# Nine norms' sums in four column groups of the array, and two stretches of vector work held in program order

## The chip, the cores and the metric

The kernel runs on one core of a Trainium2 chip. The metric is the device time of one execution in microseconds (us); less is better. Engines are called PE (matrix multiplications), DVE (vector), ACT (scalar functions and copies), POOL (a second, slower vector engine) and SP (which issues most DMA transfers). Each runs its own instructions in its own order and waits for the others through semaphores. SBUF is the on-chip memory, PSUM holds matmul results in eight banks of 128 partitions by 512 floats.

## The reference

One step of a decoder layer, in float32, over 1024 prompt tokens and 8 x 4 sample tokens, 1024 channels. Cut to what matters:

```python
def _rms(x, g):
    return x * lax.rsqrt(jnp.mean(x * x, axis=-1, keepdims=True) + EPS) * g

def _layer(x, p, attn_fn, ...):
    h = _rms(x, n_mix_pre)
    z = h @ w_in                                   # q | k | v | u
    a, k_state, v_state = attn_fn(q, k, v)         # window 128, a learned sink per head
    m, pool_state = _pool_mixer(u, ...)
    mix = jnp.concatenate([a, m], axis=-1) @ w_out
    x = x + _rms(mix, n_mix_post)
    f = _rms(x, n_ffn_pre)
    f = (jax.nn.silu(f @ w_gate) * (f @ w_up)) @ w_down
    x = x + _rms(f, n_ffn_post)
    return x + jax.nn.sigmoid(x @ w_ple_gate) * (p @ w_ple), ...

def _sink_attention(q, k, v, mask, sinks):
    s = jnp.where(mask, q @ k.T * 64 ** -0.5, -jnp.inf)
    m = jnp.maximum(s.max(-1), sink)
    e = jnp.exp(s - m)
    return (e / (e.sum(-1) + jnp.exp(sink - m))) @ v
```

There are four norms for each token. In the sample's attention ("decode") the scores of one kv head are 128 rows by 1056 keys: 8 caches of 128 and 32 new ones.

## The kernel before

**Layout.** Activations lie with channels in partitions and tokens in columns. The 1056 tokens are three groups of 352 columns; group 2 holds the decode tokens at its end. Each large GEMM is done as three products of values split in a high and a low half (`split`: ACT casts the high part, DVE subtracts it, L173 and L174): high x high, low x high, high x low, each with 128x128 weights and 352 columns on PE (L128). Names end in h and l for the halves: `fh`, `fl` are the FFN's input, `wh`, `wl` weights, `hid` and `hp` the hidden activations, `sh`, `sl` sums of weights. For groups 0 and 1 the FFN uses a scheme of seven products of sums (`seven`, `do_dn_pair`), whose sums of weights are made by POOL (L1058), and whose results DVE adds up from PSUM (L1085, L1228: `p`, `u`, `c`, `ap`).

**What sets the order.** PE's order is the order in which the program is written. Transfers by SP and PSUM banks follow it: a bank is given out in turn, and a matmul that gets one waits until the result eight banks ago has been read. DVE, ACT and POOL instructions are ordered by a scheduler at build time, except where `fix` is called while `fixed[0]` is true: then the instruction keeps its place in the program. Work that accompanies the GEMMs (norms, splits, reloads) is written as generators, called chains. After each product `turn(n)` advances a clock by n matmuls, and resumes each chain that is due; a chain says with `yield load, wait` how much DVE work it has just issued and how long it then waits, both in matmuls (0.16 us in the profile).

**Norms.** `rstd_steps(acc)` gets the squares summed down to one 128 x 352 tile. Three matmuls with `acc`'s columns as weights and one column of ones as moving data give sums in token order, 128 x 3 (the last piece overlaps). ACT takes the root, DVE the reciprocal, and splits it in halves (`hl`); two multiplies with shifted identities (`diag`) make a 128 x 384 matrix `dg` of each half, and after `yield 6, 14` two matmuls with ones as weights spread the result over all partitions. It is used twelve times: three times at the start, six in `ffn_steps`, three in `x2_steps` after the FFN.

**Decode softmax.** `dscores` makes the scores of two kv heads (`a_1322`, `a_1323`) and calls `softmax` for each: maximum, its negative `nmx`, the sink's part `es`, the exponent with its sum on ACT, sum and reciprocal on DVE, the multiply on POOL (L707). `scores` then does the same for a prompt block, of two times four heads (`a_1366`); its masked copies are an ACT copy and a DVE copy by predicate (L741, L742). `dturned` transposes the weights on PE (L122), and between these stand filler products: `out_pool`, whose result ACT copies to `y` (L844). Later come `dvalues`, in column groups of 64.

**Reload.** Group 2's FFN input was stored in DRAM. `do_reload` issues two loads of it (`fr`, 128 x 1408 each) and starts a chain which splits each into `fh` and `fl` while the last down projections of the seven products run; `do_combine` ends that stretch by finishing all chains.

Of the kernel before, what the change touches and what calls it, by code (L numbers as in the profile page):

```python
# [16 lines left out]
P = 128  # L17
# [45 lines left out]
def trunk_kernel(  # L63
# [68 lines left out]
    def bank():  # L132
        return psum.tile([P, 512], F32, tag="b", name=nm("b"))
# [218 lines left out]
            for k in range(KC)  # L352
        ]

    def rstd_steps(acc):

        n = acc.shape[1]
        sm = bank()  # L360
        for i in range(TB):
            at = min(i * P, n - P)
            mm(sm[:, i : i + 1], acc[:, at : at + P], ones[:, 0:1], start=True, stop=True)
        sd = spool.tile([P, TB], F32, tag="sd", name=nm("sd"))
        fix(se.activation(sd, sm[:, :TB], AF.Sqrt, bias=epst, scale=1.0 / D))
        fix(ve.reciprocal(sd, sd))
        hl = spool.tile([P, 2, TB], F32R, tag="hl", name=nm("hl"))
        fix(ve.tensor_copy(hl[:, 0], sd))
        fix(ve.tensor_tensor(hl[:, 1], sd, hl[:, 0].bitcast(F32), op=ALU.subtract))
        dgs = []  # L370
        dg2 = act_tile([P, 2, TB, P], F32R, "dg")
        for h in range(2):
            dg = dg2[:, h]
            fix(
                ve.tensor_tensor(
                    dg, diag, hl[:, h].bitcast(F32).unsqueeze(2).to_broadcast([P, TB, P]), op=ALU.mult
                )
            )
# [169 lines left out]

    pinned[0] = True
    norms = [None] * G  # L550
    norms[0] = rstd_steps(acc1[0])
    for h in range(2):
        for c in range(4):
            u_prod(c, 0, h)
# [11 lines left out]
    x_operand(2, 1)  # L566
    for c in range(4):
        u_prod(c, 1, 1)
    norms[1] = rstd_steps(acc1[1])
    u_norm(norms[1], 1)  # L570
    for h in range(2):
        u_prod(0, 2, h)
# [4 lines left out]
        u_evict(c, 1)  # L577
        se.copy(u_decode(c)[:, :, 0:PST], stt[:, c])
    split(wplh, wpll, wpl)
    norms[2] = rstd_steps(acc1[2])  # L580
    u_norm(norms[2], 2)
    for h in range(2):
        u_prod(1, 2, h)
# [103 lines left out]
            ve.tensor_tensor(lo[:, :, dst], src, hi[:, :, dst].bitcast(F32), op=ALU.subtract)  # L687
            at += m

    def softmax(t, nh, scale, sk, nsk):  # L690

        mx = spool.tile([P, nh], F32, tag="mx", name=nm("mx"))
        ve.tensor_reduce(mx, t, axis=AX.X, op=ALU.max)
        nmx = spool.tile([P, nh], F32, tag="nmx", name=nm("nmx"))
        ve.scalar_tensor_tensor(nmx, mx, -scale, nsk, op0=ALU.mult, op1=ALU.min)
        es = spool.tile([P, nh], F32, tag="es", name=nm("es"))
        ve.tensor_tensor(es, sk, nmx, op=ALU.add)
        se.activation(es, es, AF.Exp)
        sm = spool.tile([P, nh], F32, tag="sm", name=nm("sm"))
        for c in range(nh):  # L700
            se.activation(  # L701
                t[:, c, :], t[:, c, :], AF.Exp, bias=nmx[:, c : c + 1], scale=scale, accum_out=sm[:, c : c + 1]
            )
        ve.tensor_tensor(sm, sm, es, op=ALU.add)
        ve.reciprocal(sm, sm)
        nk = t.shape[2]
        ge.tensor_tensor(t, t, sm.unsqueeze(2).to_broadcast([P, nh, nk]), op=ALU.mult)  # L707

    def m4(i):
        return am[:, i, :].unsqueeze(1).to_broadcast([P, 4, WIN])  # L710
# [4 lines left out]
    def scores(b):  # L715


        t = act_tile([P, 8, WIN])
        nk = 2 * WIN if b else WIN
        lo = b * WIN + WIN - nk  # L720
        at = WIN * 4 // nk
        both = [[bank() for _ in range(4 // at)] for _ in range(2)]
        for c in range(4):
            for kv in range(2):
                rows = slice(64 * kv, 64 * kv + 64)
                i = c % at
                mm(
                    both[kv][c // at][:, i * nk : (i + 1) * nk],
                    qT[c][rows, b * WIN : (b + 1) * WIN],
                    kT[rows, lo : lo + nk],  # L730
                    start=True,
                    stop=True,
                )
        for kv in range(2):
            tk = t[:, 4 * kv : 4 * kv + 4, :]
            for i, ps in enumerate(both[kv]):
                tc_ = tk[:, i * at : (i + 1) * at, :]
                v = ps.rearrange("p (c k) -> p c k", k=nk)
# [7 lines left out]
            softmax(tk, 4, 0.125, skp[:, hs], nskp[:, hs])  # L746
        return t

    def turned(b, t):
# [44 lines left out]
    def dscores():  # L794
        ts = [act_tile([P, 1, NK]) for _ in range(2)]
        for lo, n in ((0, 512), (512, 512), (1024, NDEC * DSEQ)):
            for kv in range(2):
                rows = slice(64 * kv, 64 * kv + 64)
                ps = bank()
                if lo < 1024:  # L800
                    k = ckt[rows].rearrange("p b w -> p (b w)")[:, lo : lo + n]
                else:
                    k = kT[rows, SEQ:]
                mm(ps[:, :n], qd[rows], k, start=True, stop=True)
                ve.tensor_tensor(ts[kv][:, 0, lo : lo + n], ps[:, :n], dmt[:, lo : lo + n], op=ALU.add)  # L805
        for kv in range(2):
            softmax(ts[kv], 1, 0.125, skd[:, kv : kv + 1], nskd[:, kv : kv + 1])
        return ts

    def dturned(t):  # L810
# [420 lines left out]

    def do_combine():
        finish(list(chains))
        for a, b in ((2, 1), (1, 6), (7, 1), (1, 5), (1, 3), (4, 7), (7, 5)):
            ve.tensor_tensor(accp[a], accp[a], accp[b], op=ALU.add)
        os_[0] = [accp[2], accp[4]]
        os_[1] = [accp[1], accp[7]]
        for g in (0, 1):
            begun.update((g, m) for m in range(KC))
# [9 lines left out]
            nc.sync.dma_start(d, t)  # L1249

    def do_reload():
        def steps():
            ts = [half(2, s="fr") for h in range(2)]
            for h in range(2):
                nc.sync.dma_start(ts[h], fsd[h])
            yield 0, 50
            for h in range(2):
                fs[2][h] = f_operand(ts[h], 2)
                yield 10, 70

        chain(steps())

# [219 lines left out]
```

## Time and profile before

| what | value |
|---|---|
| three runs | 1088.72, 1089.14, 1089.16 us, median 1089.14 |
| the profiled execution | 1088.29 us; its span 1086.5 us |
| granted PE clock | 0.999 of full speed |
| PE busy | 1076.8 us, 99% |
| DVE, ACT, POOL busy | 873.2 (80%), 512.4 (47%), 283.2 us (26%) |
| pitch of 128x352 matmuls | 0.16 us |

The span runs from the first to the last instruction; the executed time is 1.8 us more. Rows of the timeline show the start, the duration, the engine, the line in the code, the operation, output and input by name, the shape, a count, and in brackets how long the engine had been idle and what it waited for. Matmuls are pipelined: each is shown with 0.32 us but starts 0.16 us after the one before. In the waits of PE the numbers are total us, times, and the longest. DVE is over 90% busy in several stretches of the FFN, the last of them from about 794 to 845 us, and PE waits for it in few places.

### The profile page before, as it was taken

To read this page: it belongs to the slowest core of one execution; us is meant where nothing else is said; L and a number is where in the kernel's file an instruction comes from. 1 tells how busy PE (TensorE), PEld (TensorE's weight loads), DVE (VectorE), ACT (ScalarE), POOL (GpSimd) and SP (SyncE) were. 2 spreads that over 40 slices of the span, in tenths; PEclk is the share of its full clock that TensorE was granted. 3 is DMA by queue.
4 is the path that set the end of the run, shared out by engine and by line. 5 is a ranking of instruction groups with operands and counts; after the bars stand their busy time and mean duration, and the time that the engine had idled before them with its cause. 6 is when DMAs were issued, how large, how long until landed. Compare 5 with 4: busy or idle time off the path is not lost.

```text
span 1086.5 us, 17727 instructions
## 1 busy us (share of the span) xinstructions
PE 1076.8 (99%) x6867; PEld 1060.1 (98%) x6867; DVE 873.2 (80%) x1312; ACT 512.4 (47%) x877; POOL 283.2 (26%) x212
## 2 busy tenths in 40 slices
PE   9999999999999999999999999999999999999998
PEld 8999988899999999999999999999998999999998
DVE  6777478886878956796598898898899997969973
ACT  7423277774555533345543343443344365545531
POOL 0073032200000023436545445454442000022300
PEclk9999999999999999999999999999999999999999
DMA  8121311534553432322222222212234556553461
GB/s 296 59 72 39 120 50 40 188 143 141 190 184 130 136 117 78 131 78 78 78 79 78 83 74 85 91 59 97 79 112 161 170 179 224 182 210 125 135 203 60
DMA packets 43572, 131.27 MB, mean 121 GB/s; under 512 B 5060, under 2 KB 15588, under 8 KB 43488
## 3 DMA queue, kind: packets, MB, share of 16 engines
q1 hardware_dynamic: 42160, 128.38, 34.7%
q10 hardware_dynamic: 1328, 1.77, 0.5%
q8 instruction: 54, 0.88, 0.3%
q14 instruction: 30, 0.25, 0.1%
HBM read 114.25 MB, written 15.87 MB: 120 GB/s over the span
## 4 chain that ended last, share of the span: by engine, by line
PE 95%; DVE 3%; POOL 1%; ACT 1%; issue 1%; DMA 0%; SPq 0%; DVEq 0%; POOLq 0%; ACTq 0%
PE b L128 94%; PE b L122 1%; POOL wr L1058 1%; DVE sl L174 1%; DMA xr<-in_x_dram 0%; DVE hp L174 0%; DVE a L805 0%; DVE ap L1228 0%; ACT a L701 0%; DVE wl L174 0%; DVE hf L1133 0%; POOL a L707 0%; DVE w L174 0%; ACT sh L173 0%; DVE fl L174 0%
## 5 line engine op out<-in xcount | busy, mean ns | idle before, releaser
L1058 POOL TENSOR_TENSOR wr<-wr,wr 128x512 f32<-128x512 f32 x108 | 174.0, 1625 | 482.2 <-DMA wr<-in_w_gu_dram 242.3
L173 ACT CAST wh<-wr 128x1024 fp32r<-128x1024 f32 (+1 forms) x138 | 142.1, 1031 | 164.3 <-PE b L128 92.2
L174 DVE TENSOR_TENSOR wl<-wr,wh 128x1024 fp32r<-128x1024 f32 (+1 forms) x138 | 168.1, 1219 | 51.4 <-ACT wh L173 35.4
L128 PE MATMUL b<-fh,wh 128*128 128x352 f32 x624 | 201.5, 323 | 0.0
L128 PE MATMUL b<-fh,wl 128*128 128x352 f32 x624 | 200.0, 320 | 0.0
L128 PE MATMUL b<-fl,wh 128*128 128x352 f32 x624 | 199.9, 320 | 0.0
L173 ACT CAST sh<-wr 128x1024 fp32r<-128x1024 f32 x72 | 75.7, 1051 | 138.0 <-POOL wr L1058 131.9
L128 PE MATMUL b<-fh,sh 128*128 128x352 f32 x416 | 134.3, 323 | 0.0
L128 PE MATMUL b<-fl,sh 128*128 128x352 f32 x416 | 133.2, 320 | 0.0
L128 PE MATMUL b<-fh,sl 128*128 128x352 f32 x416 | 133.2, 320 | 0.0
L174 DVE TENSOR_TENSOR sl<-wr,sh 128x1024 fp32r<-128x1024 f32 x72 | 97.5, 1356 | 36.1 <-ACT sh L173 18.2
L128 PEld LDWEIGHTS b<-fl,wh 128*128 128x128 f32 x624 | 117.4, 188 | 0.0
L128 PEld LDWEIGHTS b<-fh,wh 128*128 128x128 f32 x624 | 117.0, 188 | 0.0
L128 PEld LDWEIGHTS b<-fh,wl 128*128 128x128 f32 x624 | 116.9, 187 | 0.0
L128 PE MATMUL b<-h,wh 128*128 128x352 f32 x480 | 105.6, 326 | 0.6 <-ACT h L426 0.6
L128 PE MATMUL b<-hid,wh 128*128 128x352 f32 x416 | 99.6, 322 | 0.0
L128 PEld LDWEIGHTS b<-h,wh 128*128 128x128 f32 x480 | 82.4, 190 | 1.6 <-ACT h L426 0.9
L1058 POOL TENSOR_TENSOR wr<-wr 128x512 f32<-128x512 f32 x36 | 51.0, 1416 | 105.9 <-DVE w L174 105.9
L128 PEld LDWEIGHTS b<-fl,sh 128*128 128x128 f32 x416 | 78.2, 188 | 0.0
L128 PEld LDWEIGHTS b<-fh,sh 128*128 128x128 f32 x416 | 78.0, 188 | 0.0
L128 PEld LDWEIGHTS b<-fh,sl 128*128 128x128 f32 x416 | 77.9, 187 | 0.0
L128 PE MATMUL b<-hp,sh 128*128 128x352 f32 x320 | 76.7, 322 | 0.8 <-DVE p L1085 0.6
(195 smaller groups left out, 2245.7 us busy)
## 6 DMA issues: line engine op xcount, KB each, us to landing
wr<-in_w_gu_dram SPq DMA_DIRECT2D x88, 512.0 KB, 3.3
wr<-in_w_dn_dram SPq DMA_DIRECT2D x40, 512.0 KB, 3.2
wr<-in_w_pg_dram SPq DMA_DIRECT2D x16, 512.0 KB, 3.5
x<-in_x_dram SPq DMA_DIRECT2D x6, 704.0 KB, 9.9
x1d<-x SPq DMA_DIRECT2D x6, 704.0 KB, 3.6
x<-x1d SPq DMA_DIRECT2D x6, 704.0 KB, 5.7
out_y_dram<-yo SPq DMA_DIRECT2D x24, 176.0 KB, 1.9
wr<-in_w_out_b_dram SPq DMA_DIRECT2D x8, 512.0 KB, 3.3
```

What stands on the lines that cost most here:

```text
L122: ins = te.transpose(out, src, ident)
L128: ins = te.matmul(*args, **kw)
L173: fix(se.copy(hi, src))
L174: fix(ve.tensor_tensor(lo, src, hi.bitcast(F32), op=ALU.subtract))
L1058: ge.tensor_tensor(out, a, b, op=op)
```

## The change

**Norms.** The old function is kept as `rstd_first` for the three norms at the start. The new `rstd_steps` takes `acc` as moving data: four matmuls, each with 32 columns of ones as weights and a quarter of the tokens (88) as columns, each into its own 32 partitions of one bank. So every token's sum stands in 32 partitions. Root, reciprocal and halves are 128 x 88, and four identity columns (`lead`) pick one row of each group of 32 to build the 128 x 352 matrix. The chain yields 8, 22 there, so the two spreading matmuls stand 12 to 24 products later in some places.

**Decode softmax.** One call for both heads: first maximum, `nmx` and `es` of each, then the exponents of both, then sum, reciprocal and multiply of each, with the DVE instructions held in this order.

**Reload.** `fixed[0]` is true from `do_reload` until `do_combine`, so the two splits stand where the chain issues them, and the chain waits 75 rather than 50 matmuls after the loads, and 12 rather than 70 between the splits.

Line numbers behind the norms are 24 to 36 higher after the change (L707 becomes L739, L742 L774, L844 L875, L1228 L1261).

How the order moves on DVE in the decode softmax. `mx_1342` and the next maximum are those of the two kv heads; `b_1367` to `b_1370` are the banks of the prompt block's scores. Before:

```order
L693 TENSOR_REDUCE mx_1354<-a_1323 128x1
L695 SCALAR_TENSOR_TENSOR nmx_1344<-mx_1342,c_1290 128x1
L742 COPY_PREDICATED a_1366<-a_1280,b_1367 128x256
L697 TENSOR_TENSOR es_1346<-c_76,nmx_1344 128x1
L695 SCALAR_TENSOR_TENSOR nmx_1356<-mx_1354,c_1290 128x1
L742 COPY_PREDICATED a_1366<-a_1280,b_1368 128x256
L697 TENSOR_TENSOR es_1358<-c_76,nmx_1356 128x1
L742 COPY_PREDICATED a_1366<-a_1280,b_1369 128x256
L693 TENSOR_REDUCE mx_1383<-a_1366 128x4
L695 SCALAR_TENSOR_TENSOR nmx_1385<-mx_1383,c_1289 128x4
L704 TENSOR_TENSOR sm_1349<-sm_1349,es_1346 128x1
L705 RECIPROCAL sm_1349<-sm_1349 128x1
```

The first head's sum stood behind the first prompt maximum. Now, from the same place:

```order
L722 SCALAR_TENSOR_TENSOR nmx_1344<-mx_1342,c_1290 128x1
L774 COPY_PREDICATED a_1366<-a_1280,b_1369 128x256
L724 TENSOR_TENSOR es_1346<-c_76,nmx_1344 128x1
L720 TENSOR_REDUCE mx_1348<-a_1323 128x1
L722 SCALAR_TENSOR_TENSOR nmx_1350<-mx_1348,c_1290 128x1
L724 TENSOR_TENSOR es_1352<-c_76,nmx_1350 128x1
L736 TENSOR_TENSOR sm_1355<-sm_1355,es_1346 128x1
L737 RECIPROCAL sm_1355<-sm_1355 128x1
L736 TENSOR_TENSOR sm_1358<-sm_1358,es_1352 128x1
L737 RECIPROCAL sm_1358<-sm_1358 128x1
L774 COPY_PREDICATED a_1366<-a_1280,b_1368 128x256
L774 COPY_PREDICATED a_1366<-a_1280,b_1370 128x256
```

Both sums and reciprocals stand ahead of two of the four copies; both prompt maxima follow these copies.

The same place on ACT: the exponents of the decode head (`a_1323`), those of the prompt block (`a_1366`), and the copy of `y`, which empties the bank `b_1443`. Before:

```order
L701 ACTIVATE a_1323,sm_1361<-a_1323,nmx_1356 128x1056
L698 ACTIVATE es_1387<-es_1387 128x4
L741 COPY a_1366<-b_1370 128x256
L701 ACTIVATE a_1366,sm_1390<-a_1366,nmx_1385 128x128 x4
L844 COPY y_1287<-b_1443 128x352
L698 ACTIVATE es_1406<-es_1406 128x4
L701 ACTIVATE a_1366,sm_1409<-a_1366,nmx_1404 128x128 x4
L818 COPY a_1458<-b_1459 128x512
```

The copy of `y` stood between two fours of exponents. Now:

```order
L731 ACTIVATE a_1323,sm_1358<-a_1323,nmx_1350 128x1056
L773 COPY a_1366<-b_1368 128x256
L773 COPY a_1366<-b_1370 128x256
L173 CAST wh_1918<-wr_1225 128x1024
L731 ACTIVATE a_1366,sm_1390<-a_1366,nmx_1385 128x128 x2
L728 ACTIVATE es_1387<-es_1387 128x4
L731 ACTIVATE a_1366,sm_1390<-a_1366,nmx_1385 128x128 x2
L731 ACTIVATE a_1366,sm_1409<-a_1366,nmx_1404 128x128
L728 ACTIVATE es_1406<-es_1406 128x4
L731 ACTIVATE a_1366,sm_1409<-a_1366,nmx_1404 128x128 x3
L875 COPY y_1287<-b_1443 128x352
L849 COPY a_1458<-b_1459 128x512
```

It now stands behind all eight, and a cast of weights stands ahead of them.

The reload on ACT, where `sh_8356` is a cast of summed weights and `hid_8275` the hidden activations. Before:

```order
L173 CAST sh_8356<-wr_8154 128x1024
L173 CAST fh_8554<-fr_8458 128x1408
L173 CAST hid_8275<-c_8408 128x352
L173 CAST wh_8375<-wr_8315 128x1024
L1157 ACTIVATE p_8317<-p_8317 128x352
```

And now:

```order
L173 CAST sh_8356<-wr_8154 128x1024
L173 CAST hid_8275<-c_8408 128x352
L173 CAST wh_8375<-wr_8315 128x1024
L1190 ACTIVATE p_8317<-p_8317 128x352
```

The cast of `fr` no longer stands between the weights and `hid`; it comes seven rows further on.

The reload on DVE, at the adds of down projections (`ap`). Before:

```order
L1228 TENSOR_TENSOR ap_5237<-ap_5237,b_8531 128x352
L174 TENSOR_TENSOR fl_8555<-fr_8458,fh_8554 128x1408
L174 TENSOR_TENSOR sl_8490<-wr_8360,sh_8489 128x1024
L1228 TENSOR_TENSOR ap_5254<-ap_5254,b_8539 128x352
L1228 TENSOR_TENSOR ap_5254<-ap_5254,b_8547 128x352
```

Now at this place, and ten rows further on:

```order
L1261 TENSOR_TENSOR ap_5237<-ap_5237,b_8531 128x352
L1261 TENSOR_TENSOR ap_5254<-ap_5254,b_8539 128x352
L174 TENSOR_TENSOR sl_8490<-wr_8360,sh_8489 128x1024
L1261 TENSOR_TENSOR ap_5254<-ap_5254,b_8547 128x352
```
```order
L1261 TENSOR_TENSOR ap_5168<-ap_5168,b_8605 128x352
L174 TENSOR_TENSOR fl_8587<-fr_8458,fh_8586 128x1408
L174 TENSOR_TENSOR wl_8518<-wr_8449,wh_8517 128x1024
L1261 TENSOR_TENSOR ap_5185<-ap_5185,b_8613 128x352
L1261 TENSOR_TENSOR ap_5185<-ap_5185,b_8621 128x352
L174 TENSOR_TENSOR wl_8592<-wr_8499,wh_8591 128x1024
L174 TENSOR_TENSOR fl_8629<-fr_8459,fh_8628 128x1408
L1261 TENSOR_TENSOR ap_5216<-ap_5216,b_8639 128x352
```

The first `fl` moved behind nine of these rows, the second behind `wl_8592`.

The diff, without the rows that only rename the first three calls:

```diff
-    def rstd_steps(acc):
+    def rstd_first(acc):
...
+    def rstd_steps(acc):
+        w = acc.shape[1] // 4
+        sm = bank()
+        for j in range(4):
+            mm(sm[32 * j : 32 * j + 32, :w], ones[:, :32], acc[:, j * w : (j + 1) * w], start=True, stop=True)
+        t = act_tile([P, 10, w], F32R, "dg")
+        sd, hl = spool.tile([P, w], F32, tag="sw", name=nm("sw")), t[:, 8:10]
+        se.activation(sd, sm[:, :w], AF.Sqrt, bias=epst, scale=1.0 / D)
+        ve.reciprocal(sd, sd)
+        ve.tensor_copy(hl[:, 0], sd)
+        ve.tensor_tensor(hl[:, 1], sd, hl[:, 0].bitcast(F32), op=ALU.subtract)
+        lead = ident[:, ::32].unsqueeze(2).to_broadcast([P, 4, w])
+        for h in range(2):
+            part = hl[:, h].bitcast(F32).unsqueeze(1).to_broadcast([P, 4, w])
+            ve.tensor_tensor(t[:, 4 * h : 4 * h + 4], lead, part, op=ALU.mult)
+        yield 8, 22
+        ps = bank()
+        for h in range(2):
+            mm(ps[:, : 4 * w], ones_r, t[:, 4 * h : 4 * h + 4].rearrange("p i k -> p (i k)"), start=h == 0, stop=h == 1)
+        return ps[:, : 4 * w]
...
-    def softmax(t, nh, scale, sk, nsk):
...
+    def softmax(*parts):
+        scale = 0.125
+        held = []
+        for t, nh, sk, nsk in parts:
+            mx = spool.tile([P, nh], F32, tag="mx", name=nm("mx"))
+            fix(ve.tensor_reduce(mx, t, axis=AX.X, op=ALU.max))
+            nmx = spool.tile([P, nh], F32, tag="nmx", name=nm("nmx"))
+            fix(ve.scalar_tensor_tensor(nmx, mx, -scale, nsk, op0=ALU.mult, op1=ALU.min))
+            es = spool.tile([P, nh], F32, tag="es", name=nm("es"))
+            fix(ve.tensor_tensor(es, sk, nmx, op=ALU.add))
+            held.append((nmx, es))
+        sums = []
+        for (t, nh, _, _), (nmx, es) in zip(parts, held):
+            se.activation(es, es, AF.Exp)
+            sm = spool.tile([P, nh], F32, tag="sm", name=nm("sm"))
+            for c in range(nh):
+                se.activation(
+                    t[:, c, :], t[:, c, :], AF.Exp, bias=nmx[:, c : c + 1], scale=scale, accum_out=sm[:, c : c + 1]
+                )
+            sums.append(sm)
+        for (t, nh, _, _), (_, es), sm in zip(parts, held, sums):
+            fix(ve.tensor_tensor(sm, sm, es, op=ALU.add))
+            fix(ve.reciprocal(sm, sm))
+            nk = t.shape[2]
+            ge.tensor_tensor(t, t, sm.unsqueeze(2).to_broadcast([P, nh, nk]), op=ALU.mult)
...
+    fixed[0] = True
     td = dscores()
+    fixed[0] = False
...
     def do_combine():
         finish(list(chains))
+        fixed[0] = False
...
     def do_reload():
+        fixed[0] = True
+
         def steps():
...
-            yield 0, 50
+            yield 0, 75
             for h in range(2):
                 fs[2][h] = f_operand(ts[h], 2)
-                yield 10, 70
+                yield 10, 12
```

More of the change, by code (lines that the diff above doesn't have):

```diff
@@ L550, in trunk_kernel @@
     norms = [None] * G
-    norms[0] = rstd_steps(acc1[0])
+    norms[0] = rstd_first(acc1[0])
     for h in range(2):
@@ L568, in trunk_kernel @@
         u_prod(c, 1, 1)
-    norms[1] = rstd_steps(acc1[1])
+    norms[1] = rstd_first(acc1[1])
     u_norm(norms[1], 1)
@@ L579, in trunk_kernel @@
     split(wplh, wpll, wpl)
-    norms[2] = rstd_steps(acc1[2])
+    norms[2] = rstd_first(acc1[2])
     u_norm(norms[2], 2)
@@ L688, in put @@
             at += m
-    def softmax(t, nh, scale, sk, nsk):
[L692 to L707, printed above, removed]
+    def softmax(*parts):
[23 more added lines that the diff above has]
+            ge.tensor_tensor(t, t, sm.unsqueeze(2).to_broadcast([P, nh, nk]), op=ALU.mult)
     def m4(i):
@@ L745, in scores @@
             hs = slice(4 * kv, 4 * kv + 4)
-            softmax(tk, 4, 0.125, skp[:, hs], nskp[:, hs])
+            softmax((tk, 4, skp[:, hs], nskp[:, hs]))
         return t
@@ L805, in dscores @@
                 ve.tensor_tensor(ts[kv][:, 0, lo : lo + n], ps[:, :n], dmt[:, lo : lo + n], op=ALU.add)
-        for kv in range(2):
-            softmax(ts[kv], 1, 0.125, skd[:, kv : kv + 1], nskd[:, kv : kv + 1])
+        softmax(*((ts[kv], 1, skd[:, kv : kv + 1], nskd[:, kv : kv + 1]) for kv in range(2)))
         return ts
```

## The prediction, made before the change was run

> **What bounds the kernel now.** I read the page's shares and its chain first, then the waits of TensorE (PE), then the timeline of each engine around those waits. The page's rows of busy time and of the chain by line:
>
> ```profile
> PE 1076.8 (99%) x6867; PEld 1060.1 (98%) x6867; DVE 873.2 (80%) x1312; ACT 512.4 (47%) x877; POOL 283.2 (26%) x212
> ```
>
> PE is busy 1076.8 of 1086.5 us, so nearly everything hangs on its matmuls, and another engine matters only where PE waits for it. The view of PE's waits lists those places:
>
> ```profile
> PE b L128 <- DVE ap L1228: 1.7, 2, 1.5
> ...
> PE b L122 <- POOL a L707: 1.1, 1, 1.1
> ...
> PE b L128 <- DVE p L1085: 0.6, 1, 0.6
> ```
>
> That is 3.4 us in four stalls. L707 is the decode softmax; L1228 and L1085 lie in the stretch where group 2's operand is reloaded. The change touches both, and beside them the 0.6 us or so that PE spends on each norm's sum. So three terms, each a us or two of 1088.29 (the profiled execution; the median 1089.14 stands 0.85 above it).
>
> **Term 1, nine norm sums.** The last norm before, PE in order of time:
>
> ```profile
> 998.03 0.32 PE L128 MATMUL b<-fh,w 128*128 128x352 f32 x1
> 998.20 0.72 PE L128 MATMUL b<-c,acc 128*128 128x1 f32 x6
> 998.78 0.41 PE L128 MATMUL b<-fh,sh 128*128 128x352 f32 x1
> 999.02 0.33 PE L128 MATMUL b<-fl,sh 128*128 128x352 f32 x1
> ```
>
> Without sums, two matmuls later would be 0.32 us later (pitch 0.16); here 998.03 to 999.02 is 0.99. So a sum costs 0.67 us. The new sum is four fp32 matmuls, each two passes, in column groups of 32. No row has that form; the nearest are the attention's matmuls in pairs of groups, and their borders with full-array matmuls:
>
> ```profile
> 146.20 0.70 PE L128 MATMUL b<-a,a 64*128 64x256 f32 x4
> 148.49 0.29 PE L128 MATMUL b<-a,a 128*64 128x16 f32 x4
> 149.09 0.51 PE L128 MATMUL b<-a,a 128*64 128x16 f32 x12
> 149.53 0.43 PE L128 MATMUL b<-mh,wh 128*128 128x352 f32 x1
> 149.80 0.32 PE L128 MATMUL b<-ml,wh 128*128 128x352 f32 x1
> 154.20 0.32 PE L128 MATMUL b<-mh,wl 128*128 128x352 f32 x1
> 154.45 0.88 PE L128 MATMUL b<-a,a 128*64 128x256 f32 x4
> ```
>
> Going in: 0.25 from the last full matmul to the first of a group (154.20 to 154.45). Four records of 16 columns take 0.29, of 256 columns 0.70; a record of them lasts 0.21 and 0.38, so the second pass starts 0.08 and 0.32 behind the first: for 88 columns I interpolate 0.15, and add 0.02 for starting four groups rather than two. Going out: the last record starts about 0.14 before 149.53, 0.19 with 72 more columns; the next full matmul follows 0.27 after. Sum 0.25 + 0.02 + 0.15 + 0.19 + 0.27 - 0.32 = 0.56, a saving of 0.11 each, 1.0 us in nine. If the four groups overlapped fully and the borders cost no more than PE's 0.16 pitch, 0.4 each would be saved (-2.5 to be safe with the count); if they ran one behind the other, 3 x 0.15 more each: +3.0 in all. I take -1.0, since the pairs in the rows plainly overlap.
>
> The Trainium skill, page "TensorEngine Tiling (Array Packing)", Key Properties, says that changing the tiling mode drains TensorE, and that tiles within a mode run independently. The first half speaks against this change: nine times a mode is entered and left. By that rule the sum is the one above, and the trace agrees: 0.25 and 0.27 stand at the borders where 0.16 is the pitch.
>
> The other engines' part is off the path. The two multiplies that spread the result have this row:
>
> ```profile
> L375 DVE TENSOR_TENSOR dg<-c,hl x24: 549/551/554, 26.8 to 1002.7; 128x384 fp32r<-128x384 f32 x24
> ```
>
> That is 1.4 ns a column, so reciprocal, cast and subtraction on 88 columns rather than 3 cost 0.12 us more each, 0.4 a norm, of which the multiplies on 352 columns give back 0.1; the matmuls that spread the result stand 12 to 24 matmuls later (yields 8, 22 for 6, 14), so they have more time, not less, and PE's waits name none of the norms.
>
> **Term 2, decode softmax.** PE, POOL, DVE and ACT there:
>
> ```profile
> 138.84 0.32 PE L128 MATMUL b<-mh,wl 128*128 128x352 f32 x1
> 140.25 1.20 PE L122 MATMUL b<-c,a 128*128 128x128 f32 x9 [1.08 <-POOL a L707]
> ...
> 144.11 0.41 PE L128 MATMUL b<-mh,wh 128*128 128x352 f32 x1
> ```
> ```profile
> 138.25 1.95 POOL L707 TENSOR_TENSOR a<-a,sm 128x1056 f32<-128x1056 f32 x1 [6.58 <-ACT a L701]
> 140.78 1.95 POOL L707 TENSOR_TENSOR a<-a,sm 128x1056 f32<-128x1056 f32 x1 [0.59 <-DVE sm L705]
> ```
> ```profile
> 133.09 2.41 DVE L693 TENSOR_REDUCE mx<-a 128x1 f32<-128x1056 f32 x2
> ...
> 138.49 1.72 DVE L704 TENSOR_TENSOR sm<-sm,es 128x1 f32<-128x1 f32 x1
> ...
> 140.60 0.69 DVE L693 TENSOR_REDUCE mx<-a 128x4 f32<-128x512 f32 x1
> 141.32 1.42 DVE L695 SCALAR_TENSOR_TENSOR nmx<-mx,c 128x4 f32<-128x4 f32 x1
> ```
> ```profile
> 135.60 1.18 ACT L701 ACTIVATE a<-a,nmx 128x1056 f32<-128x1056 f32 x1 [0.65 <-DVE nmx L695]
> ...
> 136.97 1.16 ACT L701 ACTIVATE a<-a,nmx 128x1056 f32<-128x1056 f32 x1
> ...
> 140.23 0.40 ACT L701 ACTIVATE a<-a,nmx 128x128 f32<-128x128 f32 x1 [1.53 <-POOL a L707]
> ...
> 141.78 0.43 ACT L844 COPY y<-b 128x352 f32<-128x352 f32 x1
> ```
>
> The tiny DVE operations at 138.49 and 141.32 last 1.7 and 1.4 us and end with POOL's multiplies (140.20, 142.73): a small operation on SBUF alone is held while POOL runs; the reduction at 140.60 is not.
>
> In the new order the first maximum (1.2 us) ends at 134.3, its exponent starts at 134.8 instead of 135.60, and sum and reciprocal stand right behind it: POOL's first multiply starts at about 137.1, 1.1 us earlier, and PE's transposes at about 139.1 instead of 140.25. The second multiply runs 139.5 to 141.5. But the two copies of masked scores, both prompt maxima and then nmx now stand behind both sums, and nmx is held till 141.5. The eight prompt exponents, 0.38 each with two small ones, then run in one piece from 141.7 to about 145.0, and the copy of y (L844) that stood between the fours, at 141.78, stands behind all eight: 145.0 to 145.4. PE's twelve matmuls that now start at 144.11 need the bank which that copy empties. PE would reach them at 143.0 and starts them at about 145.4: +1.3 us. What comes behind on ACT (transposed copies) is wanted from 147.4 on and is done by 148.1 just ahead of its use. Bounds: -1.1 if the copy costs PE nothing (the first stall goes, no new one comes); +2.6 if the masked copies are held by POOL too, which the reduction speaks against.
>
> **Term 3, the reload.** ACT, DVE, POOL and PE:
>
> ```profile
> 815.50 1.36 ACT L173 CAST fh<-fr 128x1408 fp32r<-128x1408 f32 x1
> 816.77 0.48 ACT L173 CAST hid<-c 128x352 fp32r<-128x352 f32 x1
> ...
> 833.34 1.05 ACT L173 CAST wh<-wr 128x1024 fp32r<-128x1024 f32 x1 [2.58 <-DMA wr<-in_w_gu_dram]
> ```
> ```profile
> 817.28 0.53 DVE L174 TENSOR_TENSOR hid<-c,hid 128x352 fp32r<-128x352 f32 x1 [1.45 <-ACT hid L173]
> ...
> 823.19 2.23 DVE L1228 TENSOR_TENSOR ap<-ap,b 128x352 f32<-128x352 f32 x5
> 825.35 2.23 DVE L174 TENSOR_TENSOR fl<-fr,fh 128x1408 fp32r<-128x1408 f32 x1
> 827.50 2.32 DVE L174 TENSOR_TENSOR sl<-wr,sh 128x1024 fp32r<-128x1024 f32 x1
> ...
> 834.32 1.62 DVE L174 TENSOR_TENSOR fl<-fr,fh 128x1408 fp32r<-128x1408 f32 x1
> ```
> ```profile
> 819.43 0.58 PE L128 MATMUL b<-hp,sh 128*128 128x352 f32 x2 [0.56 <-DVE p L1085]
> ...
> 823.76 0.59 PE L128 MATMUL b<-hp,sh 128*128 128x352 f32 x2 [0.21 <-DVE ap L1228]
> ...
> 830.30 0.59 PE L128 MATMUL b<-hp,wh 128*128 128x352 f32 x2 [1.47 <-DVE ap L1228]
> ```
>
> A cast of fr stands ahead of hid on ACT; DVE idles 1.45 us for it, and PE stalls twice. Then fl and sl, 4.5 us in a row on DVE, hold the add whose bank PE wants: the third stall. PE's late starts here, with 0.1 of uncovered weight load behind each, come to 3.2 us. In the new order hid follows at once (about 1.3 us earlier), so the first two stalls go; one ap add stands ahead of sl and no fl, so the third goes: going through by these durations, DVE frees that bank at 824.6, and PE wants it at 827.3. What is late next: both fl now stand between 831 and 837, one behind wl and ahead of two ap adds that PE waits for. DVE reaches the first of these at 837.3, ends at 837.7, and PE wants the bank at 837.0: a new stall of 0.75, with its weight load 0.85. Net -2.3. Bounds: -3.2 if fl runs at 1.4 and the new stall is hidden; -0.5 if the weights that land at 833.3 land no sooner and DVE loses 2 us there. The fr loads themselves are issued by SP as before, only what uses them is later.
>
> **Sum.** -1.0 + 1.3 - 2.3 = -2.0: 1088.29 to 1086.3 profiled, and with the 0.85 above, 1087.1; I say 1087.0. About 0.2% (2.2 us) is what a measurement here can tell from no change, and the forecast lies on that border.
>
> **Rivals.**
> - The copy of y costs nothing, and the softmax gains its stall back: 1087.0 - 2.4 = 1084.6. For it: POOL surely starts earlier. Against: the order on ACT, eight exponents ahead of the copy. 0.22.
> - The groups run one after another: +4.0 on term 1, 1091.0. Against: four records in 0.29 us at 148.49. 0.10.
> - The reload does not do what it says: DVE has no idle time from 817 to 845, so stalls move and do not go: 1087.0 + 2.3 = 1089.3. For it: the same work is still on DVE before 845. Against: 1.45 us of idle time goes. 0.13.
> - Slower: every column group drains the array for itself. Then three more borders of 0.09 + 0.14 + 0.11 and three passes of 0.15 a norm, 0.8 to 1.0 each: 1087.0 + 1.0 + 9 = about 1095 by the larger; from 0.5 a norm more than before it decides. Against: groups start in pairs at 148.49. 0.08.
>
> The forecast has 0.45, with its own range 1085.4 to 1088.6; 0.02 is left. Faster: 0.22 and just over half of 0.45, so 0.46. Slower: 0.08, and 0.02 of the groups in a row, 0.10. Same: 0.44. The range of 8 in 10 goes from 1083.8 to 1090.2: it holds the rival of the free copy, the forecast and the unmoved reload.
>
> **What would show it.** Right: PE's wait for L707 gone, a new wait of PE for ACT's copy of y of about 2 us near 143; norm sums, eight records, in about 0.56 us from row to row; no PE wait for ap or p before 830 and one of under 1 us near 837. Wrong: sums above 0.67; no wait for y; or a stall behind fl longer than 1.5.

## The result: slower, and the profile after

The changed kernel took 1095.6 us (mean of five runs, 1095.2 to 1096.2), the one before 1088.76 in the same session: a ratio of 1.0063, 95% interval 1.0049 to 1.0077. The forecast was 1087.0, range 1083.8 to 1090.2. Run again in another session (e1) it took 1093.35 against 1088.98: 1.0048 (1.0031 to 1.0065). The profiled run of the first result (1914.38 us) and one run of e2 (1176.74 us) had granted clocks of 0.739 and 0.851 and are left out of all times, so the rows of after are those of e1's profiled execution: 1093.13 us, span 1091.3, clock 0.999, to be held against 1088.29 and 1086.5.

The page's busy row and the waits of PE, after:

```profile
PE 1079.2 (99%) x6885; PEld 1058.0 (97%) x6885; DVE 875.5 (80%) x1312; ACT 513.6 (47%) x877; POOL 282.3 (26%) x212
```
```profile
PE b L128 <- ACT y L875: 2.1, 1, 2.1
PE b L128 <- DVE fl L174: 2.0, 2, 1.2
...
PE b L128 <- DVE dg L403: 0.4, 1, 0.4
PE b L128 <- DVE ap L1261: 0.2, 1, 0.2
```

The waits for L1228 (now L1261), L707 and L1085 have shrunk or gone, and the wait for y has come, as forecast. The waits for fl and for dg were not forecast. And PE's busy time has grown by 2.4 us although each norm's sum is shorter: something makes PE slower where it waits for nothing. The last norm's sum, PE in order of time:

```profile
1002.85 0.32 PE L128 MATMUL b<-fh,w 128*128 128x352 f32 x1
1003.10 0.36 PE L128 MATMUL b<-acc,c 128*32 128x88 f32 x8
1003.39 0.43 PE L128 MATMUL b<-fh,sh 128*128 128x352 f32 x1
1003.65 0.32 PE L128 MATMUL b<-fl,sh 128*128 128x352 f32 x1
```

From 1002.85 to 1003.65 is 0.80 us; less two pitches of 0.16, a sum costs 0.48 us, where it was 0.67.

To see where the 4.84 us between the two profiled executions arise, I compared when PE reaches the same product in both. After less before, in us, and what lies in each stretch:

| stretch of the program (time in after) | added | made of |
|---|---|---|
| to 45 | +0.25 | start, which differs so much between any two profiles |
| 45 to 224 | +0.8 | decode softmax |
| 224 to 330 | +2.0 | PE waits for fl +2.9; five sums -1.2; pitch +0.3 |
| 330 to 877 | +0.4 | pitch of the matmuls +3.3; reload -2.7; a sum -0.2 |
| 877 to 908 | +0.9 | PE waits for dg +0.9; pitch +0.2; a sum -0.2 |
| 908 to the end | +0.5 | pitch +0.8; two sums -0.4 |

The parts are rounded and add up to within 0.2 us. Three entries are new: the waits for fl and dg, and a pitch (the time from one matmul's start to the next) that is longer by 0.7% over half the program.

**The wait for fl.** PE and DVE in after, where group 2's normalized operand (fh, fl) is made; then DVE before, and PE before at its first use of each `fl`:

```profile
271.00 0.32 PE L128 MATMUL b<-fh,wh 128*128 128x352 f32 x1
272.10 0.43 PE L128 MATMUL b<-fl,wh 128*128 128x352 f32 x1 [0.78 <-DVE fl L174]
...
274.25 0.43 PE L128 MATMUL b<-fh,wh 128*128 128x352 f32 x1
275.91 0.43 PE L128 MATMUL b<-fl,wh 128*128 128x352 f32 x1 [1.23 <-DVE fl L174]
```
```profile
269.86 0.57 DVE L1015 SCALAR_TENSOR_TENSOR y<-x,c,b 128x352 f32<-128x352 f32 x1
270.42 1.63 DVE L174 TENSOR_TENSOR fl<-y,fh 128x1408 fp32r<-128x1408 f32 x1
271.96 0.58 DVE L1015 SCALAR_TENSOR_TENSOR y<-x,c,b 128x352 f32<-128x352 f32 x1
...
274.23 1.62 DVE L174 TENSOR_TENSOR fl<-y,fh 128x1408 fp32r<-128x1408 f32 x1
```
```profile
265.84 1.63 DVE L174 TENSOR_TENSOR fl<-y,fh 128x1408 fp32r<-128x1408 f32 x1
...
269.63 1.62 DVE L174 TENSOR_TENSOR fl<-y,fh 128x1408 fp32r<-128x1408 f32 x1
```
```profile
270.37 0.32 PE L128 MATMUL b<-fl,wh 128*128 128x352 f32 x1
...
272.27 0.32 PE L128 MATMUL b<-fl,wh 128*128 128x352 f32 x1
```

PE starts a product 0.16 us after the one before; here the next start is 1.10, 0.44 (at 273.81) and 1.66 us off, and 0.27 behind two of them, 2.9 us over what five pitches take. Before, the two fl are ready at 267.47 and 271.25 and PE uses them at 270.37 and 272.27. Now both start 4.6 us later: the last scaled pieces of y (L1015) are still being made at 271.96, and the second fl starts at 274.23. The pieces of y are made from the norm's spread result; that its later place is the cause is tested in e6.

**The pitch.** PE in one window of equal length, 340 to 780 us, in the FFN, before and after (the two fences in this order). The columns are the window, its length, PE's busy time, its matmuls in brackets, granted clock, DMA share and GB/s:

```profile
340.00:780.00 440.00, 440.00 (x2771) 1.00 0.27 90
```
```profile
340.00:780.00 440.00, 440.00 (x2752) 1.00 0.27 90
```

Same clock, no wait on either side, yet 19 matmuls fewer: 440 us over 2771 is 158.8 ns, over 2752 it is 159.9. By the starts of the records alone the mean pitch is 158.89 and 160.00 ns. At some 3000 matmuls from 337 to 820 us this is 3.3 us.

### The profile page after: what moved, and what is told of

Read it like the earlier page. It is cut to its first block, busy times and chain, and to the rows that moved or that the text cites. A ratio compares the mean times of both kernels' runs of the same rounds, so it can differ in the third digit from the quotient of the medians.

```text
span 1912.6 us, 17766 instructions
## 1 busy us (share of the span) xinstructions
PE 1906.3 (100%) x6885; PEld 1604.5 (84%) x6885; DVE 853.7 (45%) x1312; ACT 524.6 (27%) x877; POOL 252.0 (13%) x212
## 4 chain that ended last, share of the span: by engine, by line
PE 72%; DVE 0%; ACT 0%; issue 0%; DVEq 0%
PE b L128 72%; DVE fl L174 0%; ACT fh L173 0%; DVE sg L1383 0%; DVE yo L1385 0%; ACT sq L884 0%; DVEq L1383 0%
## 5 line engine op out<-in xcount | busy, mean ns | idle before, releaser
L128 PE MATMUL b<-fh,wh 128*128 128x352 f32 x624 | 299.0, 479 | 0.0
L128 PE MATMUL b<-fl,wh 128*128 128x352 f32 x624 | 298.3, 478 | 0.4 <-DVE fl L174 0.4
L128 PE MATMUL b<-fh,wl 128*128 128x352 f32 x624 | 298.4, 478 | 0.0
L128 PE MATMUL b<-fh,sl 128*128 128x352 f32 x416 | 189.7, 456 | 0.0
L128 PE MATMUL b<-fl,sh 128*128 128x352 f32 x416 | 189.6, 456 | 0.0
L128 PE MATMUL b<-h,wh 128*128 128x352 f32 x480 | 189.3, 528 | 0.2 <-DVE h L452 0.2
L128 PE MATMUL b<-hid,wh 128*128 128x352 f32 x416 | 158.0, 479 | 0.0
L128 PEld LDWEIGHTS b<-h,wh 128*128 128x128 f32 x480 | 142.3, 302 | 12.6 <-issue 4.5
L128 PEld LDWEIGHTS b<-hid,wh 128*128 128x128 f32 x416 | 101.1, 246 | 17.2 <-issue 1.7
L128 PE MATMUL b<-h,wl 128*128 128x352 f32 x240 | 112.3, 530 | 0.0
```

The lines of the kernel that those rows point to most:

```text
L128: ins = te.matmul(*args, **kw)
```

## The experiments

All ratios are to the kernel before, run on the same chip in the same session. The expectations name theories by letters: A, the prediction's three terms were mis-sized; B, the column groups cost the array more than their rows show; C, a lower granted clock; D, the later spreading delays group 2's fl; E, the pitch of the 128x352 matmuls; F, the place of the spreading pair's second operand sets that pitch. D and F were shown, E in its size but not in its first cause; B was refuted, since the sums became cheaper; A holds for the sums alone, which cost less than forecast; C has a part, told at the end.

### e1 to e4: the change again, and each part alone

e1 is the change as it stands. e2 has its nine norms with their yields of 8, 22 and nothing else, e3 the softmax alone, e4 the reload alone (each the hunks of the diff above that belong to it).

> The changed kernel as it is, for a profile at full clock. Theory A (the prediction's three terms with wrong sizes): the profile shows a wait of PE for ACT's copy of y near 143 of about 2 us, sums of about 0.56 us, and stalls behind fl; together with what is gone they make +6.8 us against before. Theory B (the column groups cost the array more than their own records): nine places of PE without a named wait that lose 0.7 us or more each. Theory C (a lower granted clock, spread over everything): no stall stands out and the pitch of 128x352 matmuls is above 0.160 us.

> The kernel before with only the nine norms' sums in column groups (and their yields of 8, 22). Theory A: 1.0 us faster, at most 2.5. Theory B: 6 to 9 us slower, the whole of the change's loss. Theory C, if the clock is lost because of the groups: several us slower without a new stall.

> The kernel before with only the new softmax, its DVE instructions held in program order in the decode scores. Theory A: 1.3 us slower, from PE's wait for the copy of y; if A is to explain the whole loss by this part, 6 us or more. Theory B: 1 to 3 us slower.

> The kernel before with only the reload held in program order, with its waits of 75 and 12. Theory A: 2.3 us faster; if A is to explain the whole loss by this part, 4 us or more slower, with a stall of PE behind fl at 831 to 845. Theory B: 2 us faster.

| run | median us | ratio (95%) |
|---|---|---|
| e1 all | 1093.35 | 1.0048 (1.0031 to 1.0065) |
| e2 norms | 1094.4 (four runs) | 1.0042 (1.0024 to 1.0060) |
| e3 softmax | 1091.28 | 1.0017 (1.0007 to 1.0027) |
| e4 reload | 1085.92 | 0.9971 (0.9959 to 0.9983) |

The reload gives 3.1 us and the softmax costs about 2. Part of those 2 us is not the softmax: in e3's profiled execution its stretch, 134 to 224 us, adds 1.05 us, and 2.9 us come ahead of 45 us, where the granted clock is 0.52 from 8 to 15 us. The norms, forecast at -1.0, cost about 4.6: most of the error is there.

### e5 and e6: the new norms with the old yields, the new yields with the old norms

```diff
 # e5: nine norms in column groups
-        yield 8, 22
+        yield 6, 14
 # e6: before; the first three norms are called with (6, 14)
-    def rstd_steps(acc):
+    def rstd_steps(acc, ahead=(8, 22)):
...
-        yield 6, 14
+        yield ahead
```

> The kernel before with nine sums in column groups but the old yields of 6, 14, so the spreading matmuls stand where they stood. Two causes are open for what the norms alone lost (4.6 us): D, the later spreading matmuls, which delay group 2's fl (PE waits of about 2.8 us at 272 to 276) ; E, the pitch of the 128x352 matmuls, 160.0 ns rather than 158.9 from 345 to 830 us after the changed norms, about 3.8 us. With D alone this run is 2 us faster than before (nine sums at 0.49 instead of 0.67, the double one 0.64 instead of 1.34) with no PE wait for fl. With E as an effect of the sums it is 1 to 2 us slower than before, with a pitch of 160.0 in the FFN and no wait for fl.

> The kernel before with its old sums and only the yields of nine norms changed to 8, 22. D: about 2.5 us slower, with PE waits for fl at 270 to 276 and one for dg near 885. E by the sums: the pitch stays at 158.9 in the FFN. If E hangs on where the spreading matmuls stand, the pitch goes to 160.0 and the run is 6 us slower.

e5 took 1091.21 us (1.0029, 1.0020 to 1.0039), e6 1091.69 (1.0035, 1.0022 to 1.0048). PE's waits in e6, which has nothing of the change but that one line:

```profile
PE b L128 <- DVE fl L174: 2.0, 2, 1.2
```

It is the row of after to the digit, and e5 has no wait for fl. So the yields make that stall, without the rest of the change. In e6's trace the stretch from 270 to 280 us adds 3.0 us. In e6 the pitch stays 158.89 ns over the FFN; in e5 it is 160.00. So the pitch comes from the norms, and not from the yields.

### e7 and e8: a reset of the pitch, and one norm alone

e7 is the changed kernel with four more column-group matmuls, whose result nobody reads, right behind the last spreading pair ahead of the FFN's products (group 1's second FFN norm). e8 is before with that one norm in the new form.

```diff
         r = yield from rstd_steps(acc[g])
+        if g == 1:
+            again = bank()
+            for j in range(4):
+                mm(again[32 * j : 32 * j + 32, :88], ones[:, :32], acc[g][:, 88 * j : 88 * j + 88], start=True, stop=True)
```

> The changed kernel with four more column-group matmuls behind the last FFN norm's spreading matmuls; their result is not read. In the changed kernel every such sum was followed by a pitch of 158.9 until the next spreading matmuls. E: these 0.5 us of more work make the kernel 3 us faster than the changed one, with 158.9 from 346 to the next stall near 840. If the pitch of the FFN is set by something else (operands, addresses), it stays at 160.0 and the kernel is 0.5 us slower than the changed one.

> The kernel before with one norm in column groups, the last ahead of the FFN (group 1, second norm), old yields. One sum saves 0.18 us. E: the pitch in the FFN goes to 160.0 and this one norm costs 3 to 4 us; else the run equals the kernel before within 0.3 us.

e8 took 1091.1 us (1.0026, 1.0016 to 1.0037): no new stall, pitch 160.00, and with one norm out of nine nearly all of e5's loss. In e7 the pitch went back to 158.89 ns till 840 us, but the time, 1092.87 (1.0042, 1.0025 to 1.0059), is not better than e1's by more than the intervals. In its profiled execution PE waits 1.9 us for dg near 887 (0.43 in e1), and the granted clock is at half for some 3.4 us twice, behind 147 and behind 891 us. Its two runs at a mean clock of 0.999 took 1090.4 and 1090.6 us; e1's two at 1.000 took 1092.6 and 1092.7, in another session. The pitch's part was confirmed in the trace and not in the median.

### e9 to e11: what sets the pitch?

e9 is before, with the four unread matmuls behind the old sum of that norm. e10 is e5 with e7's reset. e11 is e10 with the reload held as in e4; its norms' ACT and DVE operations are also wrapped in `fix`, which does nothing there, since `fixed[0]` is false at all nine norms (from the first of them on it is true only between `do_reload` and `do_combine`).

> Before, with four column-group matmuls (their result is read by nobody) right behind the old sum of group 1's second FFN norm; all else, its spreading included, as before. Theory E (the pitch of 158.9 or 160.0 ns is set by the order of matmul kinds: column groups followed by a spreading pair leave the slow one, whatever the groups compute): pitch of the 128x352 matmuls 160.0 ns from about 335 to 820 us, about 2750 matmuls between 340 and 780 us instead of 2769; 0.5 us for the four matmuls and about 3.3 us for the pitch, so 1092.5, ratio about 1.0035. Rival (the slow pitch comes from the new norm's own tiles: where its 352 spreading columns lie, or what VectorE does for it): 158.9 ns as before, 2769 matmuls, and 0.5 us for the four alone, ratio about 1.0005.

> The nine norms in column groups with the old yields 6, 14 (as in e5), and four unread column-group matmuls behind the spreading matmuls of group 1's second FFN norm. Theory E: the pitch goes back to 158.9 ns from about 335 us on, 2769 matmuls between 340 and 780 us instead of 2750; 3.3 us less than e5's ratio of 1.0029, 0.5 us for the four: about 1088.4, ratio 1.0000 (0.999 to 1.001). Rival (the loss of e5 over the FFN has another cause than what stood last before it): 160.0 ns, ratio 1.0033.

> As e10, and with it the reload's splits held in program order (as in e4), and the five small operations of each of the nine norms held in program order on ACT and VectorE as the old norm's were. Left as before: decode softmax. Theory D and E with the prediction's terms 1 and 3 as measured: sums -2.0, reload -2.4, four unread matmuls +0.5, pitch of 158.9 ns over the FFN, no PE wait for fl near 271 and none for dg near 886: 1088.8 - 3.9 = 1084.9, ratio 0.9965. Rival (holding the norm's operations puts the 0.69 us reciprocal ahead of splits that PE waits for, or the pitch is 160.0 again): 1087 to 1089, ratio 0.999.

e10: 1087.67 us, 0.9998 (0.9989 to 1.0006), 2771 matmuls in the window: the reset gives back the 3.3 us. So the loss is the pitch, and it is set by what PE did last before the FFN, and stays. e9: 1088.79, 1.0008 (0.9999 to 1.0016), and 2771 matmuls. My theory E, that column groups ahead of a spreading pair leave the slow pitch, fell; the rival of that expectation, the place of the new norm's spreading columns, was left. e11: 1086.85, 0.9995 (0.9985 to 1.0004), a miss: the pitch was right, but PE waited 1.3 us for dg near 880. Its runs also part by clock: seven at 0.999 or 1.000 took 1085.5 to 1087.1 us, five at 0.996 to 0.998 took 1088.6 to 1090.5. In spite of the expectation's words, e11 says nothing on holding the norms' operations: DVE's order in it is, but for two neighbours far from there, that of e14 below, which has no such `fix`.

### e12 to e14: where the pair's second operand lies

The old norm's two spread halves begin 384 columns apart in their tile, the new norm's 352. e12 is e5 with 384, e13 is before with 352 in all twelve norms, e14 is e12 with the reload held.

```diff
 # e12
-        t = act_tile([P, 10, w], F32R, "dg")
+        t = act_tile([P, 2 * TB * P + 2 * w], F32R, "dg")
+        spread = [t[:, TB * P * h : TB * P * h + 4 * w] for h in range(2)]
...
 # e13
-        dg2 = act_tile([P, 2, TB, P], F32R, "dg")
+        dg2 = act_tile([P, 2 * TB * P], F32R, "dg")
         for h in range(2):
-            dg = dg2[:, h]
+            dg = dg2[:, n * h : n * h + TB * P].rearrange("p (i k) -> p i k", i=TB)
```

> As e5 (nine norms in column groups, yields 6, 14), with the two 352-column halves that the spreading pair reads put 384 columns apart in their tile, as in the old norm, instead of 352. Theory F (the place of the pair's second operand sets the pitch of what follows): 158.9 ns from about 335 us on, 2769 matmuls between 340 and 780 us; no unread matmuls needed; ratio 1.0000 (e5's 1.0029 less 3.3 us). Rival (another property of the new norm: the column-group sum ahead of a pair): 160.0 ns, 2750 matmuls, ratio 1.003.

> Before, with the two halves of each old norm's spread operand 352 columns apart in their tile instead of 384; the sums, yields and all else as before. Theory F: the pitch goes to 160.0 ns from about 335 to 820 us, 2750 matmuls between 340 and 780 us, no new stall: some 3.3 us slower, ratio 1.003. Rival (the old sum ahead of the pair, not the place of its operands, keeps the pitch at 158.9): 2769 matmuls, ratio 1.000.

> As e12, and the reload's splits held in program order as in e4. Left as before: decode softmax and the yields. If theory F holds: sums -2.0, reload -2.4 to -3.1, about +0.8 for PE's wait for dg near 880: 1088.2 - 3.9 = 1084.3, ratio 0.9965, below e4's 0.9971. Rival (pitch 160.0 after all): 1087.5, ratio 0.9995. A wait of PE for dg near 880 of 1.6 us as in e11 would give 1085.2, ratio 0.997.

e12 took 1085.48 us: 0.9972 (0.9962 to 0.9982). e13 took 1093.93: 1.0054 (1.0041 to 1.0066). The same window in e12, then in e13:

```profile
340.00:780.00 440.00, 440.00 (x2772) 1.00 0.26 90
```
```profile
340.00:780.00 440.00, 440.00 (x2752) 1.00 0.27 90
```

That settles which part of the norm does it. With the old sums, old yields and all else as it was, 352 columns between the halves make the pitch over the FFN 1.11 ns longer, and 384 take that away from the new norms. Whether the distance between the halves counts, or the place where the second one begins, is open: each edit moves both. e13 lost 5.6 us instead of 3.3: the pitch is 160.0 behind 890 us as well (some 1.2 us), and it has one wait for dg of 0.9 us at 230. Its two halves now overlap, as the old form writes 384 columns of each; that this makes the wait was not tested. e12 gained 2.8 us where I expected 0. Against e5's trace, beside the FFN's pitch, it saves 1.2 us for the pitch behind 890 us, 1.1 for e5's wait for dg, which it doesn't have, and 0.3 for the pitch ahead of 330 us. e14: 1086.13, 0.9976 (0.9967 to 0.9984), not the 1084.3 expected; PE waits 1.6 us for dg near 880, the case named last in its expectation. e12 and e4 both beat the kernel before and the changed one; together they give no more than either. From e12's profiled execution to e14's, the reload saves 2.5 us, the wait with its border takes 2.1, and 1.4 more go where the granted clock is at half behind that wait.

### e15 and e16: the changed kernel without the two losses

e15 is the changed kernel with halves 384 apart, e16 that with `yield 6, 14` too.

> The changed kernel with one edit: the two halves of each new norm's spread operand 384 columns apart instead of 352. Theory F with D: 158.9 ns over the FFN (2769 matmuls between 340 and 780 us), but PE still waits for fl near 271 to 275 (about 2.8 us) and for dg near 886: 1093.35 - 3.3 - 1.2 (the norms behind the FFN) = 1088.9, ratio 1.0005 (0.999 to 1.002). Rival (the rest of the change sets the pitch too, or the waits for fl cost more than shown): 1091 or more, ratio above 1.002.

> The changed kernel with two edits: halves 384 apart, and the spreading matmuls back at yields 6, 14; softmax and reload as changed. D and F: no wait for fl near 271, pitch 158.9; what is left is the prediction's three terms as measured: sums -2.0 to -2.8, softmax +1.3 to +2, reload -2.4, and up to 1.9 for a wait for dg near 880: 1084.5 to 1087.5, ratio 0.9965 to 0.999. Rival (a loss that neither D nor F names): above 1088.3.

e15: 1090.85 us, 1.0021 (1.0010 to 1.0031): 2.5 us below e1's median, less than the 4.5 expected, and just above the top of the expected ratios, 1.002. In its profiled execution the FFN's pitch is 158.89 ns, but the wait for dg is 2.3 us where e1 has 0.43. e16: 1087.11, 0.9986 (0.9976 to 0.9996), inside what was expected; without the two losses the change is a small gain. Its waits of PE:

```profile
PE b L128 <- ACT y L876: 2.1, 1, 2.1
PE b L433 <- POOL c L156: 1.6, 1, 1.6
PE b L128 <- DVE dg L404: 1.1, 1, 1.1
```

## Why the prediction was wrong, step by step

**Term 1, the sums.** The mechanism was right and the size too small: 0.49 us each against 0.67, and 0.64 against 1.34 where two norms' sums stand in one place: -2.0 us instead of -1.0. PE's record starts show why: the four groups start 6 to 7 ns apart, and the second pass 80 ns after the last of them (0.10 us after the first), where the sum had 0.02 + 0.15 us. The rivals "one after another" and "every group drains for itself" are refuted by these starts. That the second one names about 1095, near the measured time, is chance; its own terms, 1087.0 + 1.0 + 9, make 1097. The Trainium skill, page "TensorEngine Tiling (Array Packing)", Key Properties, has a change of mode drain the array; the trace agrees, with 0.25 us into the groups and 0.17 and 0.27 out of them. It was no loss.

**The step that failed** is the one on the spreading matmuls: that at yields 8, 22 "they have more time, not less, and PE's waits name none of the norms". Standing later gives DVE more time ahead of them, but what is made from their result, group 2's y, fh and fl, gets less, and the slack was too small: before, the two fl are ready 2.9 and 1.0 us ahead of PE's use of them, and they came 4.6 us later. This cost 2.9 us (e6: alone 1.0035). I looked at who waits for the input of the moved step, and not at who waits for its output.

**The second failed step** is that the norm's other work was put "off the path". In 877 to 908 us it is on it. DVE before (its three small operations and both multiplies stand in a row), DVE and PE after, and DVE in e5, which has the new norms without the held reload:

```profile
882.36 0.17 DVE L366 RECIPROCAL sd<-sd 128x3 f32<-128x3 f32 x1
...
882.84 1.02 DVE L375 TENSOR_TENSOR dg<-c,hl 128x384 fp32r<-128x384 f32 x2
```
```profile
886.11 0.69 DVE L397 RECIPROCAL sw<-sw 128x88 f32<-128x88 f32 x1
886.72 0.46 DVE L1212 TENSOR_TENSOR sl<-sl,b 128x352 f32<-128x352 f32 x1
887.10 0.19 DVE L398 CAST dg<-sw 128x88 fp32r<-128x88 f32 x1
887.21 1.22 DVE L174 TENSOR_TENSOR wl<-wr,wh 128x1024 fp32r<-128x1024 f32 x1
888.35 0.24 DVE L399 TENSOR_TENSOR dg<-sw,dg 128x88 fp32r<-128x88 f32 x1
888.51 0.95 DVE L403 TENSOR_TENSOR dg<-c,dg 128x352 fp32r<-128x352 f32 x2
```
```profile
889.08 0.86 PE L128 MATMUL b<-dg,c 128*128 128x352 f32 x2 [0.43 <-DVE dg L403]
```
```profile
885.56 0.69 DVE L397 RECIPROCAL sw<-sw 128x88 f32<-128x88 f32 x1
886.29 0.21 DVE L398 CAST dg<-sw 128x88 fp32r<-128x88 f32 x1
886.53 0.25 DVE L399 TENSOR_TENSOR dg<-sw,dg 128x88 fp32r<-128x88 f32 x1
886.70 0.95 DVE L403 TENSOR_TENSOR dg<-c,dg 128x352 fp32r<-128x352 f32 x2
```

The reciprocal on 88 columns takes 0.69 us, not 0.12 more than 0.17, and two operations for other products (sl, wl) slip in between. PE waited 0.43 us for dg, with the borders 0.9 in all. The norm's operations are not held in order here in either kernel, so this order is the scheduler's. The runs show when it comes: with the new norms and without the held reload (e2, e5, e10, e12) these operations stand in a row, as in e5's rows, and PE waits 0 to 0.6 us for dg there; with both (e1, e7, e11, e14, e15, e16) sl and wl stand between them, and PE waits 0.4 to 2.3 us; with the held reload and the old norm (e4) one sl stands between, and PE doesn't wait. So two terms that the prediction added as if apart act on each other here. Why the scheduler's order turns, what sets the length of the wait, and whether holding the norm's operations would take it away, stays open.

**What no step held** is the pitch: 3.3 us over the FFN and 1.3 outside it. The working took 0.16 us as a constant. With e12 and e13 it is shown to hang on 352 or 384 columns between the halves that the spreading pair reads.

**Term 2, softmax.** Right. PE's transposes end at 143.48 and its next product starts at 145.53, where 145.4 was forecast, behind ACT's copy of y:

```profile
142.33 1.15 PE L122 MATMUL b<-c,a 128*128 128x128 f32 x9
145.53 0.43 PE L128 MATMUL b<-mh,wh 128*128 128x352 f32 x1 [2.05 <-ACT y L875]
```
```profile
144.67 0.38 ACT L731 ACTIVATE a<-a,nmx 128x128 f32<-128x128 f32 x1
...
145.05 0.43 ACT L875 COPY y<-b 128x352 f32<-128x352 f32 x1
```

It cost +0.8 us in e1's stretch, 1.05 in e3's and about 2 in e3's median, for +1.3. The rival of the free copy is refuted. What was not foreseen is the granted clock behind such a pause (below).

**Term 3, the reload.** Right: -2.7 us in e1, -3.1 in e4's median, for -2.3. The first three stalls are gone, and the new one, forecast for 837, is there and shorter than the 0.75 forecast; here in e4 (first fence) and in after, which by then runs some 5 us behind:

```profile
838.19 0.59 PE L128 MATMUL b<-hp,sh 128*128 128x352 f32 x2 [0.31 <-DVE ap L1228]
```
```profile
843.53 0.60 PE L128 MATMUL b<-hp,sh 128*128 128x352 f32 x2 [0.22 <-DVE ap L1261]
```

The rival that the stalls would only move is refuted by e4.

So the three terms come to -2.0 + 0.8 - 2.7 = -3.9 in the trace, against -2.0 forecast. Left out were fl 2.9, pitch 4.6, dg 0.9, together 8.4, and 0.25 is the start: 4.75 of the 4.84.

## What to carry to other kernels

A step that is moved later must be followed downstream: list who reads its result and when the engine that is the bound needs that, however much time the step itself has gained. Where one engine is 99% busy, compare counts of the same instruction in equal windows as well as its waits: a pitch longer by 0.7% shows in no wait, and cost more than any stall here. Keep the layout of operands in memory the same while the way of computing them changes, or test the layout by itself.

## What the runs showed of the hardware that was not expected

**A pitch with memory.** Behind 130 us, the mean pitch of full 128x352 matmuls in fp32r, over stretches of 36, is nearly always one of three values: 158.89, 160.00 or 161.11 ns. It stays, over the FFN for some 3000 matmuls, until a norm's sum, a spreading pair, or a stall changes it. Ahead of the FFN, halves 352 columns apart leave 160.00, 384 apart leave 158.89, and four column-group matmuls put it back to 158.89. The rule has exceptions that stay unexplained: near 283 us, where two pairs stand directly behind one another, 352 leaves 158.89 as well (e5, e13), and behind a stall at a pair any of the three values was seen. Why one pair's addresses act on the matmuls behind it stays open; the granted clock is 1.00 in the windows shown.

**The clock behind a pause.** PE in e16 around the wait for y, same columns as above:

```profile
143.00:145.00 2.00, 0.69 (x7) 1.00 0.23 35
145.00:147.00 2.00, 1.25 (x7) 0.97 0.59 231
147.00:149.00 2.00, 2.00 (x8) 0.50 0.00 0
149.00:151.00 2.00, 2.00 (x14) 0.68 0.00 0
```

Behind an idle time of 2.1 us the granted clock falls to half for 3.4 us (0.03, 0.50 and 0.32 are lost in windows of 2 us), and full matmuls start 0.29 us apart instead of 0.16. Held against e1's profiled execution, which has the same idle time and no such fall, this costs 1.5 us between 146 and 152 us. The medians go with it: e16's two runs at a mean clock of 1.000 took 1084.6 and 1084.8 us, its nine at 0.998 took 1086.2 to 1088.9. The changed kernel's runs in the first session, 1095.2 to 1096.2, were all at 0.998, e1's two at 1.000 took 1092.6 and 1092.7, so about 1.5 us of the first result, and perhaps more, may come from this; that was not tested by itself. A mean clock does not say where the fall lay: in the profiled executions of e2, e3 and e15, at 0.997 and 0.998, it lies between 8 and 15 us, and not behind the later waits. The Trainium skill, page "TensorE: Matmul & The Clock Gate", Part 1, lets the clock fall to half after an idle window of about 3.4 us. Here it fell behind shorter ones, 1.6 (e14, near 880) and 2.1 us, and in e15 it did not fall behind one of 2.3 us; the measured figures decide.
